# Carrying the kept rows of a sliding-window cache through an SBUF work tile in the last layer

## Chip, cores and metric

One NeuronCore of a Trainium2 chip runs the whole program. The metric is the device time of one execution in microseconds (us). Engines are named as the profile names them: PE (matrix multiply), PEld (its weight loads), DVE, ACT and POOL (vector, scalar and general work) and SP, which here only issues DMA transfers. The core's transfers run on 16 DMA engines.

## The reference, cut to what matters

One inference step of a four-layer decoder, with a prompt of 1024 positions and a sample group of 8 sequences with 4 new positions each, so 1056 rows in all. The layers are A, B, C, A: short gated convolution, native sparse attention, RG-LRU, short gated convolution. Each ends in a matrix product, a residual and a layer norm.

```python
# layer A                                   # 4 * 1024 columns of w_in
h, b_gate, c_gate, z = split(x @ w_in, 4)
conv, new_buf = causal_dwconv(c_gate * h, buf, conv_w)
y = (silu(z) * b_gate * conv) @ w_out
# layer B, sliding branch of the sample group
all_win = concatenate([win_buf, win_new], axis=1)   # 512 cached rows, 4 new ones
nsa_win_sample = all_win[:, -512:]                  # what the next step will use
```

The change concerns the last line alone. For each of the 8 sequences, rows 4 to 511 of the cache input `cache_nsa_win` become rows 0 to 507 of the output `nsa_win_sample`. A row is 256 float32, so 508 rows are 520,192 bytes, contiguous on both sides. Nothing in the step reads that output. The 4 new rows are stored elsewhere, and the change leaves them alone.

## The kernel before

**Data.** Activations stand transposed: 8 tiles of 128 channels, each with 1056 columns in a high and a low float32r part. A product of one weight tile (1024 by 128) with three column pieces of 352 takes 3 x 24 matmuls.

**Weights.** `load_w` takes a work tile of SBUF (`wsl`, ring `ws`, 128 partitions x 1088 float32), lets SP load 512 KB into it, has ACT cast it into the high half of a tile of ring `w`, and DVE or POOL subtract to get the low half; then the work tile is free. In the second half of the program (layer B's output projection, C, and the last A) ring `ws` has 5 slots, ring `w` has 3.

**Layer A.** `layer_a` loops over 8 channel groups `c`. Each takes a work tile `g` for the convolution's input and four weight tiles, in the order 0, 2, 3, 1 (h, c_gate, z, b_gate), three column pieces each. `take` asks for weights two tiles ahead. Layer 0 runs beside a side job (`compress`: 64 indirect gathers of 1 MB from the paged cache, summed on DVE and POOL, with the rest stored again to memory); there `side` is not None. The last layer has no side job.

**Layer C.** `layer_c` runs its steps by the written order `ORDER_C`; each `gate_out(c)` ends with a DMA from memory to memory that copies the 508 kept rows of sequence `c`. Its key `("z", c)` is known to the planner only, not to the hardware.

**What sets the order.** A part of the program is recorded as steps, and `Rec.lay` plays them in a model with costs and due times (the step's number less `rec.shift`). Ring slots are handed out strictly in the order in which the steps were recorded. The resulting order is fixed for PE, ACT, DVE and POOL. SP's order is not: the framework below fills it by its own model, and an instruction without a wait on data or a slot may move far ahead. At run time each engine, SP too, takes its instructions in order, and one that waits holds back those behind it.

The first part of the program (layer A with `compress`, B's projections) is planned apart from the part that holds C and the last A.

Of the kernel before, what the change touches and what calls it, by code (L numbers as in the profile page):

```python
# [495 lines left out]
class Trunk:  # L496
# [184 lines left out]

    def out_phase(self, pm, wsrc, U, X, ln, lp, res=None, done={}, spill=None, final=None, nxt=()):

# [80 lines left out]
        for c, j in order:  # L764
# [9 lines left out]
            if (c, j) not in done:  # L774
                ps = self.mm(pm)[:, 0:TC]
                self.dense(ps, W[c], U, j, k if c else None)
                if res is None:
# [32 lines left out]

    def final_phase(self, pm, wsrc, U, X, ln, lp):

# [86 lines left out]
        for c, j in [(c, j) for c in range(4) for j in range(3)] + [(c, j) for j in range(3) for c in range(4, NCH)]:  # L899
# [3 lines left out]
            ps = self.mm(pm)[:, 0:TC]  # L903
            self.dense(ps, W[c], U, j)
            y = self.ct(TC)
# [25 lines left out]

    def put_rows(self, pm, SC, n, dests):
        nc = self.nc
        rows = self.wsl(D)
        for h in range(2):
            ps = self.aux(pm)
            for k in range(4):
                nc.tensor.transpose(ps[0:n, k * P:(k + 1) * P], SC[:, 4 * h + k, 0:n], self.idf)
            nc.vector.tensor_copy(rows[0:n, h * 512:(h + 1) * 512], ps[0:n, :])
        for a, b, dst in dests:  # L940
            nc.sync.dma_start(dst, rows[a:b, 0:D])


    def layer_a(self, pm, a, X, lp, side=None, nxt=()):
        nc, io = self.nc, self.io
        stt = nc.vector.scalar_tensor_tensor
        win = io["a_w_in"][a]
        U = [None] * NCH
        SC = lp.tile([P, NCH, 36 if self.later else 18], F32, name="SC")
        todo = [(w, c) for c in range(NCH) for w in (0, 2, 3, 1)]  # L950
        wkey = lambda x: ("a", a) + x
        wload = lambda x: self.load_w(win[:, x[0] * D + x[1] * P:x[0] * D + (x[1] + 1) * P], wkey(x))

        def take(x):

            w = self.get_w(wkey(x), lambda: wload(x))
            i = todo.index(x)
            for y in todo[i + 1:i + 3]:
                if wkey(y) not in self.pre:
                    self.pre[wkey(y)] = wload(y)  # L960
            if i >= len(todo) - 2:
                self.fetch(nxt[i - len(todo) + 2:i - len(todo) + 3])
            return w
        for c in range(NCH):
            g = self.wsl(1074)
            nc.vector.memset(g[:, 0:2], 0.0)
            gs = g[:, 1026:1074].rearrange("p (b t) -> p b t", t=6)
            nc.vector.tensor_copy(gs[:, :, 0:2], self.PT[:, c, R_SA + 16 * a:R_SA + 16 * a + 16].rearrange("p (b t) -> p b t", t=2))
            W, hs, th = {}, {}, {}

            def step(w, j):
                if w not in W:
                    W[w] = take((w, c))
                self.share(side)
                sl = slice(j * TC, (j + 1) * TC)
                np_ = TC if j < 2 else 320
                ps = self.mm(pm)[:, 0:TC]
                self.dense(ps, W[w], X, j)
                if w == 0:
                    hs[j] = self.ct(TC)  # L980
                    nc.scalar.copy(hs[j], ps)
                elif w == 2:
                    nc.vector.tensor_mul(g[:, 2 + j * TC:2 + j * TC + np_], ps[:, 0:np_], hs[j][:, 0:np_])
                    if j == 2:
                        nc.vector.tensor_mul(gs[:, :, 2:6], ps[:, 320:352].rearrange("p (b t) -> p b t", t=4),
                                             hs[j][:, 320:352].rearrange("p (b t) -> p b t", t=4))
                elif w == 3:
                    th[j] = self.ct(TC)
                    nc.scalar.activation(th[j], ps, AF.Tanh, scale=0.5)
                    stt(out=th[j], in0=th[j], scalar=1.0, in1=ps, op0=ALU.add, op1=ALU.mult)  # L990
                else:
                    u = th[j]
                    stt(out=u, in0=ps, scalar=0.5, in1=u, op0=ALU.mult, op1=ALU.mult)
                    n = TC if j < 2 else 368
                    cv = self.aux(pm)[:, 0:n]
                    o = j * TC
                    nc.scalar.activation(cv, g[:, o:o + n], AF.Copy, scale=self.par(c, R_CA + 3 * a))
                    for k in (1, 2):
                        stt(out=cv, in0=g[:, o + k:o + k + n], scalar=self.par(c, R_CA + 3 * a + k), in1=cv, op0=ALU.mult, op1=ALU.add)
                    parts = [(0, np_, cv[:, 0:np_])]  # L1000
                    if j == 2:
                        parts.append((320, 352, cv[:, 320:368].rearrange("p (b t) -> p b t", t=6)[:, :, 2:6]))
                    for a0, b0, v in parts:
                        uv, uh, ul = u[:, a0:b0], *(U[c][:, i, o + a0:o + b0] for i in range(2))
                        if a0:
                            uv, uh, ul = (q.rearrange("p (b t) -> p b t", t=4) for q in (uv, uh, ul))
                        nc.vector.tensor_mul(v, uv, v)
                        self.split(uh, ul, v, "act", "dve")
            U[c] = self.view2(self.big(F32R))
            if c == 0:  # L1010
                seq = [(w, j) for j in range(3) for w in (0, 2, 3)] + [(1, j) for j in range(3)]
            else:
                seq = [(w, j) for w in (0, 2, 3, 1) for j in range(3)]
            for w, j in seq:
                step(w, j)
            nc.vector.tensor_copy(SC[:, c, 0:2], g[:, 1024:1026])
            nc.vector.tensor_copy(SC[:, c, 2:18].rearrange("p (b t) -> p b t", t=2), gs[:, :, 4:6])
        for _ in side or ():
            pass
        self.put_rows(pm, SC, 18, [(0, 2, io["o_conv_a_prompt"][a, 0]), (2, 18, io["o_conv_a_sample"][a].rearrange("b t f -> (b t) f"))])  # L1020
        return U
# [53 lines left out]
    def layer_c(self, pm, X, lp):  # L1075
        nc, io = self.nc, self.io
        stt = nc.vector.scalar_tensor_tensor
        win = io["c_w_in"][0]
        SC = lp.tile([P, NCH, 36], F32, name="SC")
        sp, ns, hb = self.softplus(lp)  # L1080
# [99 lines left out]
        def gate_out(c):  # L1180
            h2, i = H[c // 2], c % 2
            W = self.load_w(win[:, D + c * P:D + (c + 1) * P], ("z", c))
            u = self.view2(self.big(F32R))
            U[c] = u
            for j in range(3):
                sl = slice(j * TC, (j + 1) * TC)
                ps = self.mm(pm)[:, 0:TC]
                self.dense(ps, W, X, j)
                th = self.ct(TC)
                nc.scalar.activation(th, ps, AF.Tanh, scale=0.5)  # L1190
                stt(out=th, in0=th, scalar=1.0, in1=ps, op0=ALU.add, op1=ALU.mult)
                stt(out=th, in0=th, scalar=0.5, in1=h2[:, i, sl], op0=ALU.mult, op1=ALU.mult, wk=[("z", c)])
                self.split(u[:, 0, sl], u[:, 1, sl], th, "act", "pool")

            nc.sync.dma_start(win_s[c, 0:508, :], cache[c, 4:512, :], rk=[("z", c)])
        UC, GT, WA, H = {}, {}, {}, {}
        win_s = io["o_nsa_win_sample"][0].rearrange("b t c g d -> b t (c g d)")
        cache = io["cache_nsa_win"][0].rearrange("b t c g d -> b t (c g d)")
        for x in ORDER_C.split():
            c = int(x[1])  # L1200
            if x[0] == "u":
                conv_in(c, [int(j) for j in x[2:] or "012"])
            else:
                (gates if x[0] == "g" else gate_out)(c)
# [1215 lines left out]
```

## Time and profile before

| what | us |
|---|---|
| median of 3 runs (2437.90 to 2442.79) | 2442.61 |
| profiled execution, its own time | 2450.34 |
| span of the profiled execution, first to last instruction | 2448.6 |
| PE busy in the span | 2318.3 (95%) |
| DVE, ACT, POOL busy | 1594.0, 1206.7, 955.4 |
| mean granted PE clock | 0.971 |

The rows further down are of the profiled execution. It took 7.7 us longer than the median run, so what is added to it is put on the median's scale by taking 7.7 us off. Times in rows are from the start of the span. L307 is the line of a helper that issues nearly all instructions, so rows are told apart by their tiles: `ws` a work tile, `w` a weight tile, `mm` and `aux` PSUM tiles, `x` the activations, `dd` the scratch of the norm in memory.

### The profile page before, as it was taken

What the parts mean: (1) busy time and instruction counts of PE and PEld (TensorE: products, weight loads), DVE (VectorE), ACT (ScalarE), POOL (GpSimd) and SP (SyncE); (2) the same over time, 40 slices, a digit from 0 to 9 for tenths busy, and PEclk for the clock granted to TensorE, in tenths of its full rate; (3) what the DMA queues carried; (4) which work ended last, traced back from release to release, by engine and by line L of the source; (5) the groups of instructions that cost most, each with busy time, mean ns of one, the idle gap of its engine ahead of it and who ended that gap; (6) DMA issues with size and microseconds to landing.
All of it is one profiled execution on the core that took longest, in us unless ns stands there. A gap on an engine that the chain in (4) does not pass through costs nothing. (4 is left out here: it accounts for less than half of the span.)

```text
span 2448.6 us, 41435 instructions
## 1 busy us (share of the span) xinstructions
PE 2318.3 (95%) x14801; PEld 2247.7 (92%) x14801; DVE 1594.0 (65%) x3686; ACT 1206.7 (49%) x2761; POOL 955.4 (39%) x1070
## 2 busy tenths in 40 slices
PE   8999997998989999999999999899989899999996
PEld 8999986997979889999999989899889899999996
DVE  5777865584368767777777766877873743333336
ACT  3211211244357778888888862568872432222233
POOL 3455543223148656656555542323452320000131
PEclk9999998999999999999999999999989999999998
DMA  8999987256367641111112314421204221111111
GB/s 286 352 340 350 341 273 235 90 188 219 93 204 259 249 133 50 51 35 46 43 45 68 121 44 150 137 80 44 60 26 127 83 66 52 44 41 55 35 45 71
DMA packets 334643, 320.35 MB, mean 131 GB/s; under 512 B 19462, under 2 KB 301542, under 8 KB 324964
## 3 DMA queue, kind: packets, MB, share of 16 engines
q1 hardware_dynamic: 325220, 250.58, 33.1%
q0 software_dynamic: 9216, 67.11, 7.2%
q8 instruction: 117, 1.92, 0.3%
q14 instruction: 90, 0.74, 0.1%
HBM read 237.31 MB, written 84.48 MB: 131 GB/s over the span
## 5 line engine op out<-in xcount | busy, mean ns | idle before, releaser
L307 PE MATMUL mm<-x,w 128*128 128x352 f32 x5760 | 947.9, 326 | 23.2 <-DVE c L307 9.9
L307 PEld LDWEIGHTS mm<-x,w 128*128 128x128 f32 x5760 | 937.8, 191 | 28.3 <-DVE c L307 10.4
L307 PE MATMUL mm<-big,w 128*128 128x352 f32 x2208 | 389.0, 331 | 9.9 <-ACT c L307 5.5
L307 PEld LDWEIGHTS mm<-big,w 128*128 128x128 f32 x2208 | 366.3, 193 | 13.7 <-ACT c L307 6.9
L307 POOL TENSOR_TENSOR w<-ws,w 128x1024 fp32r<-128x1024 f32 (+1 forms) x43 | 105.8, 2461 | 446.7 <-ACT w L307 426.8
L1965 DVE TENSOR_TENSOR c<-T,c 128x512 fp32r<-128x512 f32 (+1 forms) x320 | 204.8, 648 | 49.6 <-ACT c L1961 44.8
L1961 ACT CAST c<-T 128x512 fp32r<-128x512 f32 (+1 forms) x320 | 174.6, 552 | 59.5 <-PE T L1957 38.4
L307 ACT CAST w<-ws 128x1024 fp32r<-128x1024 f32 (+2 forms) x116 | 120.4, 1039 | 158.0 <-PE mm L307 122.9
L638 PE MATMUL D<-x,w 128*128 128x352 f32 x1008 | 195.4, 330 | 2.3 <-DVE big L2092 2.3
L1867 PE MATMUL A<-big 128*128 128x320 f32 (+11 forms) x832 | 181.8, 334 | 3.6 <-DVE ast L1892 1.8
L1972 PE MATMUL O<-c,big 128*128 128x256 f32 x1056 | 180.4, 291 | 0.5 <-ACT c L1961 0.2
L307 ACT CAST big<-aux 128x352 fp32r<-128x352 f32 (+3 forms) x116 | 45.7, 400 | 268.6 <-DVE aux L307 251.0
L307 DVE TENSOR_TENSOR big<-big 128x256 f32<-128x256 f32 (+3 forms) x204 | 145.9, 730 | 39.0 <-POOL big L307 35.0
L638 PEld LDWEIGHTS D<-x,w 128*128 128x128 f32 x1008 | 159.9, 188 | 5.7 <-DVE big L2092 3.5
L307 DVE TENSOR_TENSOR w<-ws,w 128x1024 fp32r<-128x1024 f32 (+2 forms) x73 | 90.9, 1245 | 110.2 <-ACT w L307 109.6
L307 POOL TENSOR_TENSOR big<-big,ws 128x1024 f32<-128x1024 f32 (+1 forms) x38 | 89.8, 2364 | 154.5 <-DMA big<-in_cache_nsa_kv,idx 69.8
L1972 PEld LDWEIGHTS O<-c,big 128*128 128x128 f32 x1056 | 147.2, 189 | 2.6 <-DVE c L1965 0.7
L1925 POOL TENSOR_SCALAR pr<-pr,G,ast 128x32 f32<-128x32 f32 (+6 forms) x192 | 126.4, 675 | 47.1 <-DVE ast L1936 42.3
L1867 PEld LDWEIGHTS A<-big 128*128 128x128 f32 x832 | 134.3, 192 | 10.4 <-PE A L1867 2.3
L307 DVE SCALAR_TENSOR_TENSOR c<-c,mm 128x352 f32<-128x352 f32 x125 | 64.3, 516 | 108.6 <-PE mm L307 53.9
L307 ACT ACTIVATE aux<-ws,PT 128x352 f32<-128x352 f32 (+2 forms) x72 | 42.6, 594 | 173.1 <-DVE ws L307 171.8
L1921 ACT ACTIVATE pr<-pr,ast 128x32 f32<-128x32 f32 (+6 forms) x192 | 118.4, 619 | 18.2 <-DVE ast L1892 17.1
(286 smaller groups left out, 4047.2 us busy)
## 6 DMA issues: line engine op xcount, KB each, us to landing
ws<-in_a_w_in SPq DMA_DIRECT2D x64, 512.0 KB
raw<-big SPq DMA_DIRECT2D x128, 256.0 KB
big<-raw SPq DMA_DIRECT2D x128, 256.0 KB
c<-dd SPq DMA_DIRECT2D x48, 176.0 KB
xs<-x SPq DMA_DIRECT2D x24, 352.0 KB
x<-xs SPq DMA_DIRECT2D x8, 1056.0 KB
ws<-in_a_w_out SPq DMA_DIRECT2D x16, 512.0 KB
ws<-in_c_w_in SPq DMA_DIRECT2D x16, 512.0 KB
```

The lines of the kernel that those rows point to most:

```text
L307: getattr(real, name)(*[f(x) for x in a], **{q: f(x) for q, x in k.items()})
L638: self.nc.tensor.matmul(ps, a, b, start=n == 0, stop=n == 23 and last)
L1867: nc.tensor.matmul(o, q[:, hl, i * P:(i + 1) * P], k, start=m == 0, stop=m == 1)
L1921: nc.scalar.activation(S[:, a:a + m], S[:, a:a + m], AF.Exp, bias=st[:, k:k + 1], scale=-1.0, accum_out=st[:, 3 + k:4 + k])
L1925: nc.gpsimd.tensor_scalar(S[:, a:a + m], S[:, a:a + m], G[:, i, 16 * k + h:16 * k + h + 1], st[:, 6 + k:7 + k], op0=ALU.mult, op1=ALU.mult)
L1961: nc.scalar.copy(x["H"][:, 0:n], x["tp"][:, 0:n])
L1965: nc.vector.tensor_sub(x["L"][:, 0:n], x["tp"][:, 0:n], x["H"][:, 0:n].bitcast(F32))
L1972: nc.tensor.matmul(O, v, M[:, y * P:(y + 2) * P], start=done[0] == 0, stop=done[0] == total - 1)
```

## The change

The eight copies leave `gate_out` of layer C. In the last layer, where `side` is None, each channel group `c` takes one more work tile right after its `g`. SP loads the 508 rows into it as 127 partitions of four rows (4 KB each), and stores them from there to the output. The two views of the tensors are now made in `layer_a`.

```diff
@@ layer_a @@
         U = [None] * NCH
+        win_s, win_c = (io[x][0].rearrange("b t c g d -> b t (c g d)") for x in ("o_nsa_win_sample", "cache_nsa_win"))
...
                         self.split(uh, ul, v, "act", "dve")
+            if side is None:
+
+                t = self.wsl(1024)[0:127].rearrange("p (t f) -> p t f", t=4)
+                nc.sync.dma_start(t, win_c[c, 4:512, :].rearrange("(p t) f -> p t f", t=4))
+                nc.sync.dma_start(win_s[c, 0:508, :].rearrange("(p t) f -> p t f", t=4), t)
             U[c] = self.view2(self.big(F32R))
@@ layer_c, gate_out @@
-
-            nc.sync.dma_start(win_s[c, 0:508, :], cache[c, 4:512, :], rk=[("z", c)])
         UC, GT, WA, H = {}, {}, {}, {}
-        win_s = io["o_nsa_win_sample"][0].rearrange("b t c g d -> b t (c g d)")
-        cache = io["cache_nsa_win"][0].rearrange("b t c g d -> b t (c g d)")
```

## Rows read from the trace of the kernel before

**Rows 1.** The page, the span in 40 slices of 61 us: PE, DMA.

```profile
PE   8999997998989999999999999899989899999996
DMA  8999987256367641111112314421204221111111
```

**Rows 2.** Stretches: us, busy (instructions) of PE, PEld, DVE, ACT, POOL; clock, DMA share, GB/s.

```profile
60.00:120.00 60.00, 60.00 (x375) 60.00 (x374) 43.51 (x70) 12.06 (x21) 26.87 (x15) 1.00 1.03 350
...
300.00:360.00 60.00, 53.99 (x324) 53.70 (x323) 45.01 (x67) 10.34 (x19) 29.31 (x16) 0.94 0.87 282
360.00:420.00 60.00, 51.26 (x296) 50.03 (x294) 32.02 (x58) 9.17 (x17) 16.99 (x11) 0.94 0.80 250
...
2048.26:2094.53 46.27, 46.27 (x290) 46.27 (x289) 16.71 (x33) 9.85 (x18) 0.00 (x0) 1.00 0.17 46
```

**Rows 3.** The copies: SP's issue ns min/median/max, first and last start us.

```profile
L307 SPq DMA_DIRECT2D out_nsa_win_sample<-in_cache_nsa_win x8: 660/705/1540, 24.0 to 228.3; - x8
```

**Rows 4.** PE in order of time, 285 to 490 us; in brackets idle time and its releaser.

```profile
328.06 40.82 PE L307 MATMUL mm<-x,w 128*128 128x352 f32 x240 [6.01 <-DVE c L307]
372.73 24.94 PE L307 MATMUL mm<-x,w 128*128 128x352 f32 x144 [3.84 <-DVE c L307]
...
429.80 1.02 PE L307 MATMUL aux<-idf,SC 128*18 128x128 f32 x4 [11.34 <-DVE big L307]
```

**Rows 5.** Waits of POOL, 285 to 435 us: total, times, longest.

```profile
POOL big L307 <- DMA big<-in_cache_nsa_kv,idx: 20.4, 5, 5.8
```

**Rows 6.** Waits of ACT, 2000 to 2320 us, the last layer: total, times, longest.

```profile
ACT w L307 <- PE mm L307: 83.8, 28, 3.4
```

**Rows 7.** DMA in two stretches, 24 to 34 and 2000 to 2300 us: packets; queue.

```profile
DMA packets 2144, 1.65 MB, mean 165 GB/s; under 512 B 67, under 2 KB 2108, under 8 KB 2128
...
DMA packets 26018, 13.38 MB, mean 45 GB/s; under 512 B 400, under 2 KB 26000, under 8 KB 26000
...
q1 hardware_dynamic: 26000, 13.11, 15.6%
```

**Rows 8.** DMA, 2327 to 2332 and 1834.5 to 1839 us: packets; SP's issues around the latter.

```profile
DMA packets 36, 0.07 MB, mean 15 GB/s; under 512 B 18, under 2 KB 18, under 8 KB 36
...
DMA packets 1213, 0.73 MB, mean 162 GB/s; under 512 B 40, under 2 KB 1177, under 8 KB 1213
...
1831.92 0.37 SPq L307 DMA_DIRECT2D ws<-in_c_w_out  x1
1833.12 0.29 SPq L307 DMA_DIRECT2D out_lru_conv_prompt<-ws  x1
1833.45 0.33 SPq L307 DMA_DIRECT2D out_lru_conv_sample<-ws  x1
```

**Rows 9.** DMA, 3.2 to 5.5 us (loads) and 2443.5 to 2447 us (stores): packets, queue's share.

```profile
DMA packets 252, 0.90 MB, mean 392 GB/s; under 512 B 32, under 2 KB 32, under 8 KB 252
...
q1 hardware_dynamic: 252, 0.90, 102.5%
...
DMA packets 527, 0.91 MB, mean 260 GB/s; under 512 B 82, under 2 KB 82, under 8 KB 527
...
q1 hardware_dynamic: 527, 0.91, 76.4%
```

**Rows 10.** The chain of waits around 1600 us: start, us, what (issue to landing).

```profile
1600.72 3.96 DMA ws<-in_c_w_in
```

**Rows 11.** SP in order of time, 1953 to 1977 us: start, us, what.

```profile
1954.05 0.38 SPq L307 DMA_DIRECT2D ws<-in_a_w_in  x1
1954.49 2.47 SPq L307 DMA_DIRECT2D c<-dd  x5
```

**Rows 12.** One weight tile's cast on ACT and its subtraction on DVE: start, us.

```profile
2094.53 1.05 ACT L307 CAST w<-ws 128x1024 fp32r<-128x1024 f32 x1 [2.32 <-PE mm L307]
...
2095.61 1.23 DVE L307 TENSOR_TENSOR w<-ws,w 128x1024 fp32r<-128x1024 f32 x1
```

**Rows 13.** PE at the end of the last layer's first product, 2324 to 2327 us.

```profile
2325.62 1.03 PE L307 MATMUL aux<-idf,SC 128*18 128x128 f32 x8
```

## The prediction

> **What bounds the kernel now.** I read the page's 40 slices first, then stretches of the two stages that the change touches, then who waits there, then the transfers themselves. PE is at 8 or 9 tenths nearly everywhere; the DMA engines are full only in the first six slices, about 360 us, and at 1 or 2 tenths at the end [rows 1]. The change takes transfers out of the first place and puts them in the second.
>
> *The first layer.* The copies are recorded in layer C, yet SP issues them between 24.0 and 228.3 us [rows 3]: nothing that the hardware knows holds them back. From 60 to 300 us the DMA engines are full at about 350 GB/s while PE hardly stops; from 300 to 420 us PE loses 14.75 of 120 us [rows 2]. Its stops end with a DVE instruction (the three shown of six, 21.2 of 26.8 us) [rows 4], and DVE and POOL stand behind the side job's gathers (POOL 20.4 us on them) [rows 5]. So a transfer less before 300 us can shorten stops after it.
>
> *The last layer.* One channel group takes 46.27 us, all of it PE at full clock, with DMA at 0.17 [rows 2]. Casts of weights wait for PE to free a `w` slot, 28 times, and for no transfer [rows 6]. The first product ends with the transposes at 2325.62 [rows 13]. PE is the bound, and any weight tile that comes late stops it once PSUM is full, for the casts share ACT's queue with the evacuation of PSUM.
>
> **What is removed.** Eight copies of 0.52 MB are 4.16 MB, at 350 GB/s 11.9 us of the first layer's transfers. The gain lies between 0 (PE hardly stops there, and past 300 us the share is 0.87 and less) and 11.9 us (the stops of 26.8 us shrink by all of it). I take 5, since about half of the stops lie where transfers still run at over 0.8. In layer C eight issues on SP go; SP waits there for others, so I count nothing. The planner's numbers shift by one per step removed, which may swap neighbours in C: between -3 and +3 us, taken as 0.
>
> **What is added: on how many DMA engines?** Of all that follows, this decides. Every transfer ends with a small packet on each engine that it used, so small packets count engines. 25 weight loads of 128 rows left 400, 16 each [rows 7]. The stores of 2 and 16 rows left 18 [rows 8]. Of the 40 between 1834.5 and 1839 us, 16 belong to the weight load issued at 1831.92, and 24 to the stores of 3, 24, 1 and 8 rows that `put_rows` of layer C makes: 3 + 12 + 1 + 8 [rows 8]. So 24 rows went over 12 engines, two each, not over 16. And one old copy, 508 rows contiguous on both sides, left 16 packets of over 8 KB (2144 less 2128) [rows 7]: it was cut into 16 equal parts, 31.75 rows each, since 508 does not divide by 16. Shares are equal in every row that I can find. The new transfers have 127 partitions, and 127 is prime: equal shares leave one engine with 127 packets of 4 KB. The other reading, whole rows rounded up (2 each for 24 rows, so 8 each for 127 and 16 engines busy), fits the 12 as well, but it would not have cut the copy through its rows. I put 0.8 on one engine.
>
> The Trainium skill, "DMA: Bandwidth & Descriptors", section "Why a DMA increments its semaphore by 16 and not by 1", speaks against this change: for SP's transfers the number of engines is the largest up to 16 that divides both sides' slowest dimension, and it names 127 partitions as a case of 1. The trace's 24 rows on 12 engines agree; no row here shows 127.
>
> **The price of one engine.** The loads from 3.2 to 5.5 us ran at 392 GB/s, 24.5 per engine, with all engines full [rows 9]: 520,192 bytes take 21.2 us. The stores at the end moved 0.91 MB in 76.4% of 16 x 3.5 us, 21.3 GB/s each [rows 9]: 24.4 us. For the store I take 22 us, nearer to the load since its packets are as large (4 KB; the end's are 2 KB). What lies around a transfer: a weight load took 3.96 us from issue to landing [rows 10], and 25 of them used 15.6% of 300 us [rows 7], 1.87 us per engine each, so 2.1 us are fixed; I take as much for a store. One trip is (21.2 + 2.1) + (22 + 2.1) = 47.4 us, between 46.6 and 49.8.
>
> The skill's same page, section "Specifications", gives about 27 GiB/s per engine; an estimate from it is 17.9 us each way, a trip of 40.0 and in the sum below about +39 in place of +98. The rows are slower, 24.5 GB/s at best, and decide.
>
> **What waits for it.** The store on SP waits until the load has landed, 23.3 us, and every weight load behind it on SP waits too. All of SP's packets are of one queue, q1 [rows 9]; I take it that each engine serves it in order, so once issued, those loads stand behind the store's 127 packets on the engine that carries a sixteenth of each of them. The planner reckons with 7 us for load and store (size over 360, 2 us each, its own figures in `Rec.lay`), so it hands the slot on to the next weight tile (w 3 of the same group) soon after, and that load can't start before the store has landed. The four other slots hold `g` or weights. In steady state I see this round:
>
> - load and store of `t`: 47.4 us;
> - the group's w 3 and w 1 loaded, back to back: 2 x 1.87 + 2.1 = 5.9 us;
> - cast 1.05 and subtraction 1.23 [rows 12], which free the slot that the next `t` gets: 2.3 us.
>
> Sum 55.6 us, where PE needs 46.27: the round is the bound. The recorded order puts the first `t` into the slot that at 1954.05 takes a weight load [rows 11]. Seven rounds later the last `t` starts at 1954.05 + 389.2 = 2343.2; it is done at 2390.6; w 3 is ready 4.0 + 2.3 us later, 2396.9; PE still has w 3, w 1 and a piece of the tile before, 7 x 3.86 = 27 us. The product ends at 2423.9, not at 2325.62: +98 us. Its last stage then runs as before. The five loads for the norm behind 1954.05 [rows 11] come up to 21 us later as well; that falls in the first round, so it is not added.
>
> **Sum.** 2450.34 + 98 - 5 = 2543.3 for the profiled execution; less 7.7 us it is 2535.6, say 2535 on the median's scale.
>
> **Rivals.**
> 1. *The spread works (other side).* If 127 rows go over 16 engines in shares of 8, each transfer has 8 x 4 KB per engine, 1.3 us at 24.5 GB/s, and 3.4 us with its fixed part. The slot is taken for 7 us of 46.27, and the DMA share rises from 0.17 by 2 x 1.3 / 46.27 = 0.06. Casts never waited for a transfer [rows 6], so the last layer stays, and the 0 to 11.9 us of the first remain: 2431 to 2443, by the 5 above 2438. It decides from the number of engines: at 4 a trip is 2 x (5.3 + 2.1) = 15 us, which the 46.27 still hide; at 1 they do not. For it: whole rows fit the 12. Against: the copy cut through rows.
> 2. *One engine, but no chain.* If SP's order puts the weight loads ahead of the store and the slot goes to another tile, only the engine is shared: 21.2 + 22 + 4 x 1.87 = 50.7 us per group against 46.27. Then eight `t` and the weights end at 1954.05 + 8 x 50.7 = 2359.7, but PE needs not wait for the last store (22 us) and has up to 27 us of work behind: +39; with idle engine time between, up to 60. About 2485, between 2455 and 2500. For it: SP's order isn't planned by hand. Against: the framework places a DMA when its model has it ready, and the store is ready early there.
> 3. *One engine and worse.* Stores at 24.4 us, and stops that start with the norm's loads 21 us late: rounds of 58.0 us give 1954.05 + 406 + 49.8 + 33.3 = 2443, +117; with the 21 added +138: 2555 to 2580.
> 4. *The change does nothing for the first layer:* 0 in place of -5. That moves every case by 5 us and decides only in rival 1 between faster and same.
>
> **How the numbers follow.** A run of this kernel can tell about 0.2%, 5 us, from no change. Chances: the chain 0.60 (2500 to 2555), no chain 0.17, worse 0.05, the spread 0.18. The last splits into faster by more than 5 us (0.10), same (0.06) and slower (0.02, through swapped neighbours). So faster 0.10, same 0.06, slower 0.84. The three cases on one engine hold 0.82, and their bounds make the range: 2455 to 2580.
>
> **What would show it.** Right: in the last layer SP's issue of the store stands some 23 us behind its load; weight loads come in bunches after a store; ACT casts wait for DMA; PE's share between 2000 and 2320 us falls to about 0.83, and the granted clock with it; small packets of a store of 127 rows number 1. In the first layer the copies are gone and the stops after 300 us shorten by some 5 of 26.8 us. Wrong: 16 small packets per new transfer, and casts that still wait for PE alone; then rival 1 holds. Wrong in size: rounds much under or over 55.6 us, which the times of the stores give directly.

## The result and the profile after

The changed kernel takes 2542.99 us (median of 6 runs, 2540.82 to 2545.28); the kernel before, run beside it, 2442.70 (6 runs, 2436.72 to 2447.99). The ratio is 1.0413, with a 95% interval of 1.0397 to 1.0429: 100 us slower. The prediction was 2535, and 2455 to 2580.

The page after, 40 slices of 63.5 us: PE, the granted clock, DMA.

```profile
PE   9999988989899899999999998998898578798996
PEclk9999989999999999999999999999998789999998
DMA  8999986185467621111123144212131111221211
```

Against [rows 1], PE has lost its row of nines in slices 31 to 37, the last layer, and the clock falls there as well. The DMA row is hardly higher there: the engines as a whole are nearly empty where the time is lost. The page's chain (shares of the span) and one of its costly groups (busy, mean ns, idle time and releaser) say what is waited for:

```profile
PE mm L307 12%; DMA ws<-in_cache_nsa_win 7%; DMA out_nsa_win_sample<-ws 5%; DVE c L307 3%; DVE big L307 2%; DMA ws<-in_a_w_in 2%; ACT c L307 1%; DMA c<-dd 1%; ACT w L307 1%; DVE aux L307 1%; DVE ws L307 1%; PE aux L307 1%; DVE w L307 1%; DVE x L307 1%; ACT L307 1%
```

```profile
L307 ACT CAST w<-ws 128x1024 fp32r<-128x1024 f32 (+2 forms) x116 | 120.4, 1039 | 283.1 <-DMA ws<-in_a_w_in 201.1
```

The two new transfers stand in the chain with 12% of the span. The same stretch of ACT as in [rows 6], 2000 to 2320 us, now waits first for weight loads:

```profile
ACT w L307 <- DMA ws<-in_a_w_in: 129.4, 5, 31.9
...
ACT w L307 <- PE mm L307: 26.2, 9, 3.4
```

SP from 2115 to 2173 us, start and duration, answers to [rows 11]. It is one round: the load of `t`, its store 21.9 us later, four weight loads in a bunch 22.3 us after that, and the next `t`.

```profile
2117.24 0.25 SPq L307 DMA_DIRECT2D ws<-in_cache_nsa_win  x1
2139.14 0.26 SPq L307 DMA_DIRECT2D out_nsa_win_sample<-ws  x1
2161.40 4.17 SPq L307 DMA_DIRECT2D ws<-in_a_w_in  x4
2171.88 0.25 SPq L307 DMA_DIRECT2D ws<-in_cache_nsa_win  x1
```

The chain of waits through the same round (start, us, what; beside [rows 10]):

```profile
2117.24 21.88 DMA ws<-in_cache_nsa_win
2139.12 0.02 issue
2139.14 22.25 DMA out_nsa_win_sample<-ws
2161.39 0.02 issue
2161.40 4.28 DMA ws<-in_a_w_in
...
2165.79 1.05 ACT w L307
...
2168.84 0.82 ACT c L307 x2
2169.65 0.95 ACT w L307
```

No step of it is long computation: 44.1 of 54.64 us are the trip. Of the four loads only the first stands in this chain. The second cast comes at 2169.65, the subtraction behind it ends at 2171.86, and the next `t` follows. DMA from 2145 to 2160 us, while only the store runs, and from 2124 to 2161.4 us, which holds the ends of one load and one store (beside [rows 7, 8]):

```profile
DMA packets 97, 0.40 MB, mean 26 GB/s; under 512 B 0, under 2 KB 0, under 8 KB 97
...
q1 hardware_dynamic: 97, 0.40, 6.4%
...
DMA packets 224, 0.92 MB, mean 25 GB/s; under 512 B 2, under 2 KB 2, under 8 KB 223
```

6.4% of 16 engines is one engine, and the small packets of two transfers are two: one each. The engine moves a 4 KB packet every 15 / 97 = 0.155 us, 26.5 GB/s; 127 of them take 19.6 us.

PE's stops in the last layer, in order of time (beside [rows 4]; the others, alike, end at 2169.35, 2224.27, 2278.58, 2333.39 and 2388.25, with 5.0 to 7.1 us):

```profile
1996.16 0.66 PE L307 MATMUL mm<-x,w 128*128 128x352 f32 x1 [24.18 <-ACT x L307]
2060.07 47.88 PE L307 MATMUL mm<-x,w 128*128 128x352 f32 x288 [13.97 <-ACT c L307]
2114.71 47.88 PE L307 MATMUL mm<-x,w 128*128 128x352 f32 x288 [6.75 <-ACT c L307]
```

A round is a stop of 6.75 and a group of 47.88 us. The group is 1.6 us longer than the 46.27 of [rows 2]: the stretch of one round shows why, by its clock, and so do the first 2.3 us of its group and the 44 us after (columns as in [rows 2]).

```profile
2117.24:2171.88 54.64, 47.88 (x290) 47.59 (x290) 16.22 (x33) 9.46 (x17) 0.00 (x0) 0.94 0.20 58
```

```profile
2114.71:2117.00 2.29, 2.29 (x8) 2.29 (x9) 1.02 (x1) 1.59 (x3) 0.00 (x0) 0.50 0.33 82
2118.00:2162.00 44.00, 44.00 (x276) 44.00 (x275) 12.51 (x24) 5.58 (x10) 0.00 (x0) 1.00 0.06 24
```

Right after the stop of 6.75 us the granted clock is 0.50, 1.2 GHz, the lower of PE's two levels; from 2118 us on it is 1.00 again. The stretches right after the other five stops of the kind show 0.50 too. From the end of layer C to the last `put_rows` (1826.2 to 2420.3 us) the trace after takes 594.1 us, that of before 494.9 (1833.1 to 2328.0): the loss is all in the last layer.

### The profile page after: what moved, and what is told of

Its sections match the earlier page's. It is cut to its first block, busy times and chain, and to the rows that moved or that the text cites. A ratio compares the mean times of both kernels' runs of the same rounds, so it can differ in the third digit from the quotient of the medians.

```text
span 2540.9 us, 41445 instructions
## 1 busy us (share of the span) xinstructions
PE 2333.6 (92%) x14801; PEld 2258.5 (89%) x14801; DVE 1596.7 (63%) x3686; ACT 1202.6 (47%) x2761; POOL 951.2 (37%) x1070
## 5 line engine op out<-in xcount | busy, mean ns | idle before, releaser
L307 PE MATMUL mm<-x,w 128*128 128x352 f32 x5760 | 968.6, 330 | 102.1 <-ACT c L307 53.1
L307 PEld LDWEIGHTS mm<-x,w 128*128 128x128 f32 x5760 | 954.1, 194 | 111.8 <-ACT c L307 55.4
L307 DVE TENSOR_TENSOR big<-big 128x256 f32<-128x256 f32 (+3 forms) x204 | 161.7, 808 | 33.4 <-POOL big L307 29.1
L307 POOL TENSOR_TENSOR big<-big,ws 128x1024 f32<-128x1024 f32 (+1 forms) x38 | 92.4, 2432 | 148.6 <-DMA big<-in_cache_nsa_kv,idx 63.6
```

Of the source, the lines that this page charges most:

```text
L307: getattr(real, name)(*[f(x) for x in a], **{q: f(x) for q, x in k.items()})
```

## The experiments

The theory: 127 partitions leave one DMA engine, so a trip takes 44 us; the weight loads wait for it through SP's order and the slot. Rivals: the work tile itself costs, or the place, or only the shared engine. Diffs are against the kernel after where nothing else is said; each ratio is against the kernel before, run on the same chip.

**128 partitions.**

```diff
-                t = self.wsl(1024)[0:127].rearrange("p (t f) -> p t f", t=4)
-                nc.sync.dma_start(t, win_c[c, 4:512, :].rearrange("(p t) f -> p t f", t=4))
-                nc.sync.dma_start(win_s[c, 0:508, :].rearrange("(p t) f -> p t f", t=4), t)
+                t = self.wsl(1016)
+                nc.sync.dma_start(t, win_c[c, 4:512, :].rearrange("r f -> (r f)").rearrange("(p f) -> p f", p=128))
+                nc.sync.dma_start(win_s[c, 0:508, :].rearrange("r f -> (r f)").rearrange("(p f) -> p f", p=128), t)
```

> The same trip through the work tile, but the 508 rows laid out as 128 partitions of 1016 floats in place of 127 of 1024. Theory (127 partitions leave one DMA engine, and the trip of 44 us on it is the loss): each of the two transfers leaves 16 completions, lands in 3 to 4 us, the stops of the last layer go, and the time is 2436 to 2443 us. Rival (the work tile itself costs: its place among the weight slots, SP's wait for the load ahead of the store, and the two transfers more, whatever the number of engines): the casts still wait for weight loads, and the time stays above 2490 us.

Measured: 2445.45 us, ratio 1.0010 (0.9999 to 1.0021). Loads land after 3.5 to 3.7 us. DMA from 2055.86 to 2063 us, one load and one store of `t`, and ACT's waits from 2000 to 2320 us:

```profile
DMA packets 288, 1.04 MB, mean 146 GB/s; under 512 B 32, under 2 KB 32, under 8 KB 288
```

```profile
ACT w L307 <- PE mm L307: 84.0, 28, 3.4
```

The small packets are 32 for two transfers, and the casts wait for PE again, as in [rows 6]. The same bytes through the same slot at the same place cost nothing measurable: the rival of the work tile is out, and the number of engines decides. The time is 2 us above the upper end expected, which had counted on a gain in the first layer; the runs without copies, below, show none.

**Fewer engines than 16, more than one.** The tile of 127 rows in two transfers each way: 122 + 5 rows, and 124 + 3 rows.

```diff
+                for a0, b0 in ((0, 122), (122, 127)):
+                    nc.sync.dma_start(t[a0:b0], win_c[c, 4 + 4 * a0:4 + 4 * b0, :].rearrange("(p t) f -> p t f", t=4))
```

(and the same for the store; in the other kernel 124 stands for 122)

> Each way in two transfers, of 122 and of 5 rows of the tile. Theory of equal shares (a divisor of the number of partitions): 122 rows go over 2 engines, 61 packets of 4 KB each, so 11 us a way, and 5 rows over 5 engines; the trip is 23 us and the round 31 us, under PE's 46.27, so the chain goes and only the late loads of the norm in the first round may cost up to 11 us: 2438 to 2452. Rival that whole rows are rounded up (8 rows on each of 16 engines): small packets number 16 and 5, the transfer lands in 4 us. Rival that the work tile costs whatever the engines: above 2490.

> Each way in two transfers, of 124 and of 3 rows of the tile. Theory of equal shares: 124 rows go over 4 engines, 31 packets each, so 31 x 0.159 + 1.7 = 6.6 us a way and a trip of 13 us; all of it hidden except some of the norm's loads in the first round: 2441 to 2450 us, less than the 2458 of two engines. Rival (it is the number of waits and transfers on SP): as with 122 and 5, 2453 to 2461.

Measured: 122 + 5 gives 2458.28 us, ratio 1.0053 (1.0034 to 1.0072), 124 + 3 gives 2450.76, ratio 1.0027 (1.0015 to 1.0039). DMA from the issue of one load to that of its store, first of 122 + 5, then of 124 + 3:

```profile
DMA packets 135, 0.54 MB, mean 44 GB/s; under 512 B 7, under 2 KB 7, under 8 KB 134
```

```profile
DMA packets 135, 0.54 MB, mean 65 GB/s; under 512 B 7, under 2 KB 7, under 8 KB 134
```

Seven small packets are 2 + 5 engines in the one and 4 + 3 in the other, not 16. On two engines a load lands after 11.7 to 12.1 us. On four the store is issued 7.5 to 8.2 us after its load, and what waits for the store 9.5 us or more after that: the trip takes 17 us there, not 13. Equal shares hold, and the rival "whole rows, rounded up" is out. After 1992 us, before their third trip, both kernels have no stop in the last layer's first product, and from the fourth trip on their loads of `t` come 46.27 us apart, PE's own pace. What is left is 15 and 7.6 us. Around the first trip PE stops for 6.3 and 2.2 us in all (the longest 3.9 and 1.6) where it didn't before, and on two engines the clock is 0.91 from 1980 to 2020 us, where before had 1.00. On four engines the rest of the 7.6 us is not found in one place. The times are 6 and 1 us over the upper ends expected: the first round was priced too low.

**Only the load.** The store is left out.

```diff
-                nc.sync.dma_start(win_s[c, 0:508, :].rearrange("(p t) f -> p t f", t=4), t)
```

> Only the loads into the work tile, on one engine as in the kernel after; the stores are left out, so the kept rows of win_sample are not written. Theory (it is the trip of load and store, 44 us with the weight loads queued behind, that exceeds what 46.27 us per group can hide): the round falls to 21.9 + 5.9 + 2.3 = 30 us, the steady stops of 5 to 7 us go, and at most the first round costs something, 2443 to 2455 us. Rival (one such transfer of 22 us is enough to hold up the weights): stops in each round, above 2480.

Measured: 2458.30 us, ratio 1.0058 (1.0038 to 1.0078). SP, 1945 to 2120 us:

```profile
1950.16 0.25 SPq L307 DMA_DIRECT2D ws<-in_cache_nsa_win  x1
1972.31 0.39 SPq L307 DMA_DIRECT2D ws<-in_a_w_in  x1
1972.75 2.47 SPq L307 DMA_DIRECT2D c<-dd  x5
...
2070.77 0.25 SPq L307 DMA_DIRECT2D ws<-in_cache_nsa_win  x1
2092.81 4.04 SPq L307 DMA_DIRECT2D ws<-in_a_w_in  x4
2117.04 0.25 SPq L307 DMA_DIRECT2D ws<-in_cache_nsa_win  x1
```

A round of 30 us is hidden: from the fourth trip on, rounds are 46.27 us. But the first weight load that wants `t`'s slot holds SP for 22 us, and the norm's five loads, which have nothing to do with it, stand behind: 1972.75 instead of 1954.49 [rows 11], though this trace reaches the last layer 3 us earlier. PE stops there for 7.5 us and, soon after, for 1.1 and 2.0, and the clock is 0.87 from 1980 to 2020 us. It has no other stop in that product that the kernel before lacks, so the 15 us of the whole kernel are put down to this place.

**The first trip left out.**

```diff
-            if side is None:
+            if side is None and c:
```

> The trip is left out for the first of the eight sequences (its kept rows of win_sample are not written); the other seven are as in the kernel after. Theory (a chain of rounds of 54.7 us from the first trip on): the stops of 24.2 and 14.0 us near 1996 and 2060 us go, the first trip starts near 1979 us, the last 6 x 54.7 later, at 2307 instead of 2336, so the time is 29 us less than after, 2510 to 2518, with steady stops of 5 to 7 us. Rival (most of the loss comes from the first trip, which holds up the norm's loads): below 2480.

Measured: 2513.68 us, ratio 1.0295 (1.0273 to 1.0316). The trips start 53.4 to 55.6 us apart, the first at 1974.94 and the last at 2303.46; after a first stop of 14.7 us at 2025.82, stops of 6.1 to 7.3 us stand before each group. The theory's number is met within its range. So the chain, once it runs, costs the same in each round, whatever the first one does.

**The tile from another ring** than the weight slots.

```diff
-                t = self.wsl(1024)[0:127].rearrange("p (t f) -> p t f", t=4)
+                t = self.big()[0:127, 0:1024].rearrange("p (t f) -> p t f", t=4)
```

> The work tile comes from the ring of large tiles instead of the five weight slots; transfers as in the kernel after, 127 partitions. Theory A (the chain goes through the slot: the weight load that gets it waits for the store to land): without it only the engine is shared, 21.9 + 22.2 + 7.5 = 51.6 us per group in place of 54.7, so 7 x 3.1 = 22 us less than after, about 2521, and not below 2490, since 51.6 is still over 46.27. Theory B (the engine's queue in order and SP's order alone make the chain): rounds stay at 54 to 55 us and the time at 2538 to 2548.

Measured: 2514.24 us, ratio 1.0281 (1.0259 to 1.0302). SP from 1935 to 2062 us, then PE's stops, then the stretch from 2062 to 2326 us:

```profile
1941.96 0.25 SPq L307 DMA_DIRECT2D big<-in_cache_nsa_win  x1
...
1965.16 8.72 SPq L307 DMA_DIRECT2D big<-in_cache_nsa_win  x1
...
2007.66 12.67 SPq L307 DMA_DIRECT2D c<-dd  x5
```

```profile
1970.85 2.69 PE L307 MATMUL aux<-ones_m,big 128*128 128x1 f32 x12 [19.64 <-DVE big L307]
2034.36 4.77 PE L307 MATMUL mm<-x,w 128*128 128x352 f32 x12 [39.78 <-ACT c L307]
```

```profile
2062.00:2326.00 264.00, 264.00 (x1645) 264.00 (x1644) 95.66 (x185) 56.55 (x98) 0.00 (x0) 1.00 0.20 62
```

Theory A's sign holds, 29 us less than after where 22 were expected, but not by its sum. From 2062 us PE never stops at all, at full clock: later trips lie 48.1 us apart, and the lag of 1.9 us per group does not reach PE (that weights loaded ahead cover it is not shown). All of the 71 us is at the start, where a free ring lets two trips begin within 23 us of each other and the norm's loads come at 2007.66. So the slot makes the steady chain. That SP's order and the shared engine make the loss at the start is read from these rows; no run separates the two.

**The place without the tile**: one copy memory to memory at the new place.

```diff
+                nc.sync.dma_start(win_s[c, 0:508, :], win_c[c, 4:512, :])
```

> The new place without the work tile: in the last layer, where the trips stand, each sequence's rows are copied memory to memory in one transfer, as the kernel before does elsewhere. Theory: the copy is cut into 16 equal parts, no transfer waits for another and no slot is taken, so the last layer stays: 2440 to 2446 us. Rival (the place costs: 0.5 MB more per channel group among the weight loads of a layer that PE fills): casts wait for weight loads there, above 2450 us.

Measured: 2442.88 us, ratio 0.9997 (0.9985 to 1.0008). PE's stops from 1834 us on add up to 12.0 us, in the trace of before to 11.9. The place costs nothing and, out of the first layer, gains nothing.

**The tile without the place**: the trip of the kernel after, recorded at the old place in layer C (against the kernel before).

```diff
-            nc.sync.dma_start(win_s[c, 0:508, :], cache[c, 4:512, :], rk=[("z", c)])
+            t = self.wsl(1024)[0:127].rearrange("p (t f) -> p t f", t=4)
+            nc.sync.dma_start(t, cache[c, 4:512, :].rearrange("(p t) f -> p t f", t=4))
+            nc.sync.dma_start(win_s[c, 0:508, :].rearrange("(p t) f -> p t f", t=4), t, rk=[("z", c)])
```

> The other part of the change alone: the trip through the work tile with 127 partitions, but recorded at the old place, the end of each channel's gate step of layer C. Theory (one engine, a trip of 44 us, SP waiting in order in the middle of it, wherever it stands): a loss again, 2460 to 2560 us, with loads landing after 22 us and casts that wait for weights in the layer where the trips run. Rival (only the last layer, where PE is full, can't hide it): 2438 to 2450.

Measured: 2643.37 us, ratio 1.081 (1.079 to 1.083): twice the loss, far above the range expected. Two of PE's stops between 1600 and 2040 us (others are as long, up to 30.4), and SP's longest waits there:

```profile
1656.27 6.53 PE L307 MATMUL mm<-x,w 128*128 128x352 f32 x26 [22.72 <-ACT ws L307]
1728.74 3.89 PE L307 MATMUL mm<-big,w 128*128 128x352 f32 x12 [22.20 <-ACT c L307]
```

```profile
SPq L307 <- DMA ws<-in_cache_nsa_win: 155.6, 8, 23.3
SPq L307 <- DMA out_nsa_win_sample<-ws: 112.1, 6, 22.0
```

Each wait of SP is as long as in the kernel after; the stops shown are over three times as long. Eight trips fill 1602.79 to 2022 us, 52 us each, where the kernel before gets from there to the stores at the end of layer C (1833.1 us) in 230 us, 29 us for each of the eight. By these numbers the same trip costs more where there is less work beside it. It also shows that a wait binds a transfer to its place: the old copies, with nothing to wait for, were issued from 24 us on [rows 3]; this one, with a slot to wait for, from 1602.79.

**The first layer.** The kept rows not moved at all (the block `if side is None:` taken out); and seven of the eight old copies made twice (against the kernel before).

```diff
             nc.sync.dma_start(win_s[c, 0:508, :], cache[c, 4:512, :], rk=[("z", c)])
+            if c:
+                nc.sync.dma_start(win_s[c - 1, 0:508, :], cache[c - 1, 4:512, :], rk=[("z", c)])
```

> The kept rows of win_sample are not moved at all: neither the old copies nor the new trips, so this part of the output is left out. What remains against the kernel before is the relief of the first layer alone. Theory: a gain of 3 to 5 us there, 2437 to 2440 us. Rival that the first layer gains nothing, since PE hardly stops there: 2442 to 2443. Upper bound, all of 11.9 us: 2431.

> The kernel before with seven of the eight old copies made twice (3.64 MB more of the same transfers in the first layer; the second copy writes the same rows again). If time in the first layer hangs on the bytes that its DMA engines move, as the prediction's 5 us assumed, 3.64 MB more at 350 GB/s cost up to 10.4 us and by the same share of one half some 4 to 5: 2447 to 2453 us. Rival (the copies only fill time that the gathers' own sequence leaves, so neither taking them away nor doubling them moves the end): 2441 to 2446.

Measured: without any transfer 2443.61 us, ratio 0.9995 (0.9983 to 1.0008), so the relief is between a loss of 2 and a gain of 4 us, and 5 is out. With seven copies more 2451.58, ratio 1.0028 (1.0016 to 1.0040), 4 to 10 us of loss. The copies of the latter on SP (issue ns, first and last start), beside [rows 3]:

```profile
L307 SPq DMA_DIRECT2D out_nsa_win_sample<-in_cache_nsa_win x15: 564/692/3700, 24.4 to 393.7; - x15
```

The doubled copies reach into the stretch after 300 us where most of PE's stops are; the eight of before ended at 228.3, where PE hardly stops. So taking copies away gained nothing, while adding some cost a little. That the place makes the difference is not shown: the trace with the doubled copies ends layer 0 at 435.4 us, only 1.6 us after the first trace of before, and copies moved to one or the other stretch alone were not run.

**Before, once more.**

> The kernel before, unchanged, for a second trace of it. If the 2 to 6 us by which the traces of the variants reach the end of the first layer earlier than the first trace of before are a difference between executions and not the work of the change, this trace too reaches it between 427 and 434 us, and its time differs from 2450.34 by about as much as its first layer does.

Measured: 2447.64 us, 2.7 less than the first trace of before. Its layer 0 ends (`put_rows` of `out_conv_a_prompt`) at 432.6 us instead of 433.8, and the traces of the variants lie at 427.1 to 435.8, with and without the old copies. So the 3.2 us by which the trace after reaches that point earlier (430.6) lie within what executions differ by; they are no measure of a gain. The second trace does not explain all of the first one's 2.7 us by the first layer (1.2).

## Why the prediction was right, step by step

- **One engine**: shown. 127 rows leave one small packet, 122 leave 2, 124 leave 4, 128 leave 16, and the loads land after some 21.9, 11.9, 7.7 and 3.6 us. The Trainium skill, "DMA: Bandwidth & Descriptors", section "Why a DMA increments its semaphore by 16 and not by 1", gives these numbers by its divisor; the traces agree in all four.
- **The trip**: 44.1 us, predicted 47.4 and at least 46.6. The rate of the rows used, 24.5 GB/s with all engines full [rows 9], was too low: one engine alone moved 26.5. The Trainium skill, the same page, section "Specifications", states about 27 GiB/s per engine; the prediction's estimate from it was 17.9 us a way. The 127 packets took 19.6, between that and the 21.2 from the rows.
- **The rest of the round**: 10.5 us, predicted 8.2. The second cast does not follow the first: it stands on ACT behind the evacuation of PSUM and comes at 2169.65. That the two errors nearly cancel, 54.6 against 55.6 us, is luck.
- **The slot hands the wait on**: shown by the other ring, where the steady stops vanish. Rival 2 (only the engine shared, 50.7 us per group) was too dear by its own sum: that case ran at 48.1, and PE did not feel it.
- **The norm's loads, "up to 21 us late as well; that falls in the first round, so it is not added"**: late they were, but not for nothing. The first one, issued right behind the first store, landed 22.38 us later, at 1991.78; the store had landed just before, for SP issued the weight load that waits for it at 1991.39. That agrees with the prediction's "each engine serves it in order". The norm behind it held PE up until 1996.16, and PE the cast that frees the slot of the second `t` (at 2006.76). The first link in the chain of waits:

```profile
1969.40 22.38 DMA c<-dd
```

  The first round, from 1947.18 to 2009.09, took 61.9 us, 6.3 more than the 55.6 put for it: the term left at nothing. The six rounds after it took 54.5 us each, 6.8 less in sum. That the two misses cancel is luck as well.
- **Where the time goes**: some 46 of the 99 us are lost before 2060 us (the group that starts at 2060.07 comes that much later after the end of layer C than its like in the trace of before), in the stops of 24.2 and 14.0 us and the work at low clock after them (clock 0.64 from 1980 to 2020 us). The six rounds after that lose 6 x (54.7 - 46.27) = 50.6 us, and the part of a group that is left 3. The prediction reached the sum by the date of the last trip and never named the clock as a term; the trips fix the dates, so it needed none. Its sign, a PE share of about 0.83 between 2000 and 2320 us, came out at 279.33 of 320 us, 0.87: work at the lower clock counts as busy.
- **The last trip** starts at 2335.92 (predicted 2343.2), 388.7 us after the first (predicted 389.2), and the product ends at 2418.0 (2423.9): +92.4 against the trace of before. The trace of before reached the last layer 7 us later than this one, so the last layer's own loss is 594.1 - 494.9 = 99.2 us, against +98.
- **The first layer, 5 us**: wrong; rival 4's 0 holds. The step that failed is "about half of the stops lie where transfers still run": the copies removed did not lie there, and fewer bytes before 230 us did not shorten the later stops: PE is busy for 104.97 of the 120 us from 300 to 420 us, before for 105.25 [rows 2]. Of the 8 us between 2535 and 2543 this term is 5, and the last layer's 99.2 instead of 98 one more; the other 2 are within the interval of the ratio.

## What to carry to other kernels

Before a transfer is put through SBUF, look at its number of partitions: 127 rows leave one engine, 128 partitions of 1016 floats carry the same bytes 6 times as fast, and the small packets at a transfer's end count its engines (in every transfer looked at here). A slow transfer costs by what is queued behind its wait, on SP and on the slot, and not by its bytes: a DMA share of 0.20 and a loss of 100 us stand side by side here. The transfers taken out of a full DMA stretch gave nothing back here, where PE hardly stopped in it.

## What was not expected of the hardware

SP's own issue of a transfer can be long. The norm's first load, issued right behind the first store, held SP for 8.54 us, where all five together took 2.47 us before [rows 11]:

```profile
1969.40 8.54 SPq L307 DMA_DIRECT2D c<-dd  x1
```

The four weight loads behind the second store took 8.51 and 9.76 us for the first two. It is seen where 127 packets for one engine lie ahead and more loads follow at once. In the kernels of 122 + 5 and 124 + 3 rows the longest issue of a store took 7.96 and 3.60 us; in the kernel with 16 engines such issues took 0.4 to 0.8 us. What inside the chip makes SP wait there, no run tells.
